# The heads stage of an RWKV-7 layer: gate projection moved, one identity matmul replaced by a VectorE add, dense k-tiles in rounds of three

## The chip, the cores and the metric

The kernel runs on one core of a Trainium2 chip. A core has five engines with their own instruction streams: TensorE (PE in the profile, its weight loads PEld), VectorE (DVE), ScalarE (ACT), GpSimd (POOL) and SyncE (SP, which here only issues DMAs). The engines wait for each other through semaphores; each works through its own instructions in a fixed order. The metric is the device time of one execution in microseconds (us), as a median of several runs.

## The reference

Two layers over 256 tokens of width 2048. Layer 0 mixes tokens by a short gated convolution, layer 1 by RWKV-7 time mixing; each is followed by a ConvFFN of width 5632. The part that matters here is the time mixing, with 32 heads of 64:

```
r, k, v = xr @ w_r, xk @ w_k, xv @ w_v
decay   = exp(-exp(-softplus(-(w0 + tanh(xw @ w1) @ w2)) - 0.5))
a       = sigmoid(a0 + (xa @ a1) @ a2)
g       = sigmoid(xg @ g1) @ g2
step:  S = S * w_t + (S @ -kk_t) (kk_t * a_t)^T + v_t k_t^T;   y_t = S @ r_t
y = groupnorm(y) * gn_g + gn_b + (sum(r * k * r_k)) * v
out = (y * g) @ w_o
```

So w, a and g each end in a product of a narrow hidden row (96, 96 and 256 wide) with a matrix of 2048 columns: these are the low-rank projections. The scan over 256 tokens is done in chunks of 64, which needs, for each head and chunk, the inverse of a 64x64 triangular matrix.

## The kernel before, in words

All products that need float32 accuracy are made of three matmuls in a reduced float32 form: a weight is split by ACT into a high part and by DVE into a low part (split_w, L136 and L137), and mm3 (L145 to L147) multiplies high by high, high by low and low by high. Weights come by SP in pieces of 1 MB into three raw buffers, and their two parts go into four buffers named hl.

The heads stage (rwkv_heads) works on pairs of heads: 16 pairs, called heads below, each 128 columns wide, on both halves of the 128 partitions. Four generators are its stages:

- stage0: the low-rank projections of w and a (tile "tl"), then 16 k-tiles of r and 16 of k into one PSUM bank "big" (group_a, which yields after every fourth k-tile: eight yields), and a copy to kr. These are the dense matmuls, 128x128 by 256 columns.
- stage1: norms of k, exponentials, and the four small products between the scaled a, b, k and r (tiles AR and BK). Its first matmul, L628, sums the squares.
- stage2: the inverse. Five levels double the inverted block. A level has two halves with a yield behind each: first X times L, scaled and masked on DVE into Tt (L711 and L713); then new X and new W in one bank of 512 columns, each made of an identity matmul that brings in the old value (L718) and eight 64x64 matmuls (L721), and one ACT copy of both to WX (L723). Then a correction (L728 to L743) gives W32.
- stage3: the matrix QT (L750, L752), the masked products FE (L757 and L759, masked on DVE at L762), the recurrence over four chunks (L772, L774), the output, group norm, the low-rank projection of the gate (gT, L802) and the product zf.

At step s, stage3 works on head s-3, stage2 on s-2, stage1 on s-1 and stage0 on s. Within a step the generators are called in turn, stage3 first, until all are done: one turn is a round. Stage2 has twelve rounds; stage0 has ten.

The code's order is only a priority: a list scheduler places instructions on each engine, and they keep that order on the chip. It can put a later round's dense matmul ahead, or break up a group. PSUM has eight banks: two each of the names "big", "tl", "inv" and "mn". The pool kx has two buffers a name, k1 one.

In the profile, AM and BR lie in a tile named xr0 (here xr_10226) and QT and FE in xr1 (xr_10227), so "mn<-xr,xr" at L759 is QT times BR, and "xr<-mn" at L762 is FE. The last three steps, with no stage0 left, are filled with the output projection's matmuls.

Of the kernel before, what the change touches and what calls it, by code (L numbers as in the profile page):

```python
# [11 lines left out]
F32 = mybir.dt.float32  # L12
# [69 lines left out]
def trunk(ctx: ExitStack, tc: tile.TileContext, x, ng, vec, cst, gnp, win, wout, up0, dn0, wl1, wv, wr, wk, wl2, wo,  # L82
# [87 lines left out]
    def group_a(src, xs, ps, j, cut=None):  # L170

        kt = 0
        ps = ps.rearrange("p (b t) -> p b t", b=NB)
        for hl in load_w(src, 1024 if KT >= 8 else KT * P, cut=cut):
            for i in range(min(8, KT)):
                c = i * P
                xh, xl = xs(kt, j)
                mm3(ps, hl[:, 0, c:c + P], hl[:, 1, c:c + P], xh, xl, kt == 0, kt == KT - 1)
                kt += 1
                if kt % 4 == 0:  # L180
                    yield
# [382 lines left out]
    def rwkv_heads(scr, xk, xr, lhid, ctxv, fill):  # L564
# [4 lines left out]
        with tc.tile_pool(name="kz", bufs=1, reuse_waits="tile") as zp, tc.tile_pool(name="kx", bufs=2, reuse_waits="tile") as kx, \  # L569
# [8 lines left out]
            def stage0(g, st):  # L578
                st.tw = kx.tile([P, T], F32, name="tw")
                st.ta = kx.tile([P, T], F32, name="ta")  # L580
                hl = load_w(wl2[g][:, :2 * P], 2 * P)[0]
                ps = bank("tl", 2, T)
                for w, dst in ((0, st.tw), (1, st.ta)):
                    mm3(ps[:, w], hl[:, 0, w * P:(w + 1) * P], hl[:, 1, w * P:(w + 1) * P], lhid[:, w, 0, :], lhid[:, w, 1, :],
                        True, True)
                    nc.scalar.activation(dst, ps[:, w], AF.Tanh, scale=0.5, bias=hb[:, w, g:g + 1])
                yield
                ps = bank("big", 2, T)
                yield from group_a(wr[g], xsel(xr), ps[:, 1], 0)
                yield from group_a(wk[g], lambda kt, j: (xk[kt // 4][:, :, kt % 4, 0, :], xk[kt // 4][:, :, kt % 4, 1, :]),  # L590
                                   ps[:, 0], 0)
                st.kr = kx.tile([P, 2, T], F32, name="kr")
                nc.scalar.activation(st.kr, ps, AF.Copy)
                yield
# [21 lines left out]
            def stage1(g, st):  # L616
# [47 lines left out]
                st.LM = kx.tile([P, NCC, CH], F32, name="LM")  # L664
# [32 lines left out]
            def stage2(g, st):  # L697
# [8 lines left out]
                WX, LT, LL = st.WX, st.LT, st.LL  # L706

                for li in range(len(LEVELS)):
                    ps = bank("inv", NCC, CH)
                    for c, s, R in pairs:  # L710
                        nc.tensor.matmul(ps[R, c], LT[R, c], WX[R, 1, c], start=True, stop=True)  # L711
                    Tt = kx.tile([P, NCC, CH], F16, name="Tt")
                    nc.vector.scalar_tensor_tensor(Tt, ps, 1.0 / NRES, bc(C_LV + 64 * li), ALU.mult, ALU.mult)  # L713
                    yield
                    ps = bank("inv", 2, NCC, CH)
                    for w in (1, 0):
                        for s, R in halves:
                            nc.tensor.matmul(ps[R, w], i16[R], WX[R, w], start=True, stop=False)  # L718
                        for c, s, R in pairs:
                            a, b = (WX[R, 0, c], Tt[R, c]) if w else (Tt[R, c], WX[R, 0, c])  # L720
                            nc.tensor.matmul(ps[R, w, c], a, b, start=False, stop=c == NCC - 1)  # L721
                    WX = kx.tile([P, 2, NCC, CH], F16, name="WX")
                    nc.scalar.activation(WX, ps, AF.Copy)  # L723
                    yield
# [4 lines left out]
                for s, R in halves:  # L729
                    nc.tensor.matmul(ps[R], i16n[R, 1], WX[R, 1], start=False, stop=False)  # L730
                for c, s, R in pairs:
                    nc.tensor.matmul(ps[R, c], LT[R, c], WX[R, 1, c], start=False, stop=False)
                    nc.tensor.matmul(ps[R, c], LL[R, c], WX[R, 1, c], start=False, stop=c == NCC - 1)
# [4 lines left out]
                for s, R in halves:  # L738
                    nc.tensor.matmul(ps[R], i16n[R, 0], WX[R, 0], start=True, stop=False)
                for c, s, R in pairs:  # L740
                    nc.tensor.matmul(ps[R, c], R16[R, c], WX[R, 0, c], start=False, stop=c == NCC - 1)
                st.W32 = kx.tile([P, NCC, CH], F32, name="W32")
# [3 lines left out]
            def stage3(g, st):  # L746
# [69 lines left out]
                nc.vector.tensor_tensor(out=grp(zf), in0=pt, in1=grp(gT), op=ALU.mult)  # L816
# [320 lines left out]
```

## Time and profile before

| what | value |
|---|---|
| median of three runs | 2610.01 us (2609.38 to 2610.29) |
| profiled execution | 2611.74 us, span 2610.0 us |
| PE busy | 2555.8 us, 98% of the span |
| DVE busy | 1696.1 us, 65% |
| ACT busy | 1348.1 us, 52% |
| granted TensorE clock | 0.995 |
| one step of the heads stage (L628 to L628) | 29.90 us |

The heads stage runs from about 1290 to 1790 us of the span. Times in the rows are in us from the span's start. In the timeline a row has its start, the time from the start of its first to the end of its last instruction, engine, line, operation, tiles, shape and count; for PE, "64*64" or "128*128" is the part of the array that a matmul uses. Matmuls overlap in the array, so that the distance of two starts, not the duration, is what one holds PE for. A group row ends with its busy time, the mean in ns of one instruction and the idle time before it.

### The profile page before, as it was taken

What the parts mean: (1) busy time and instruction counts of PE and PEld (TensorE: products, weight loads), DVE (VectorE), ACT (ScalarE), POOL (GpSimd) and SP (SyncE); (2) the same over time, 40 slices, a digit from 0 to 9 for tenths busy, and PEclk for the clock granted to TensorE, in tenths of its full rate; (3) what the DMA queues carried; (4) which work ended last, traced back from release to release, by engine and by line L of the source; (5) the groups of instructions that cost most, each with busy time, mean ns of one, the idle gap of its engine ahead of it and who ended that gap; (6) DMA issues with size and microseconds to landing.
All of it is one profiled execution on the core that took longest, in us unless ns stands there. A gap on an engine that the chain in (4) does not pass through costs nothing.

```text
span 2610.0 us, 44129 instructions
## 1 busy us (share of the span) xinstructions
PE 2555.8 (98%) x18284; PEld 2197.5 (84%) x18284; DVE 1696.1 (65%) x2365; ACT 1348.1 (52%) x2068; POOL 189.1 (7%) x255
## 2 busy tenths in 40 slices
PE   7999999999999999989999999999999999999998
PEld 7888888888888888868888888877888888888886
DVE  5666566667666645578756666665677776775555
ACT  5444455555555544469744444443555555554444
POOL 0000010000000000030222222320100000000000
PEclk9999999999999999999999999999999999999999
DMA  7555554555555555536523332335455555555553
GB/s 250 182 192 190 188 187 148 191 190 183 192 188 184 192 190 183 223 131 213 183 81 105 105 95 92 105 111 211 161 194 189 185 191 194 191 184 194 194 194 141
DMA packets 107417, 450.00 MB, mean 172 GB/s; under 512 B 29808, under 2 KB 47872, under 8 KB 57296
## 3 DMA queue, kind: packets, MB, share of 16 engines
q1 hardware_dynamic: 105760, 440.52, 48.1%
q0 software_dynamic: 1456, 6.66, 0.7%
q8 instruction: 143, 2.34, 0.3%
q14 instruction: 58, 0.48, 0.1%
HBM read 439.15 MB, written 8.00 MB: 171 GB/s over the span
## 4 chain that ended last, share of the span: by engine, by line
PE 76%; issue 18%; DVE 3%; ACT 1%; POOL 1%; DMA 0%; SPq 0%; DVEq 0%; POOLq 0%; ACTq 0%
PE tl L199 6%; PE big L199 6%; PE inv L199 6%; PE mn L199 6%; PE big L145 5%; PE big L146 4%; PE big L147 4%; PE tl L200 3%; PE big L200 3%; PE inv L200 3%; PE mn L200 3%; PE tl L145 2%; PE tl L147 2%; PE tl L146 2%; PE mn L146 2%
## 5 line engine op out<-in xcount | busy, mean ns | idle before, releaser
L137 DVE TENSOR_TENSOR hl<-raw,hl 128x1024 fp32r<-128x1024 f32 (+1 forms) x820 | 977.8, 1195 | 503.3 <-ACT hl L136 500.2
L136 ACT ACTIVATE hl<-raw 128x1024 fp32r<-128x1024 f32 (+1 forms) x820 | 843.5, 1031 | 575.9 <-PE big L147 151.0
L199 PE MATMUL big<-xhl,hl 128*128 128x512 f32 x880 | 309.4, 392 | 0.0
L199 PE MATMUL tl<-xhl,hl 128*128 128x512 f32 x880 | 309.4, 392 | 0.0
L199 PE MATMUL mn<-xhl,hl 128*128 128x512 f32 x864 | 303.9, 392 | 0.0
L199 PE MATMUL inv<-xhl,hl 128*128 128x512 f32 x864 | 303.6, 392 | 0.0
L200 PE MATMUL big<-xhl,hl 128*128 128x256 f32 x880 | 246.0, 280 | 0.0
L200 PE MATMUL tl<-xhl,hl 128*128 128x256 f32 x880 | 246.0, 280 | 0.0
L200 PE MATMUL mn<-xhl,hl 128*128 128x256 f32 x864 | 241.5, 279 | 0.0
L200 PE MATMUL inv<-xhl,hl 128*128 128x256 f32 x864 | 241.4, 279 | 0.0
L199 PEld LDWEIGHTS big<-xhl,hl 128*128 128x128 f32 x880 | 164.8, 187 | 38.0
L199 PEld LDWEIGHTS tl<-xhl,hl 128*128 128x128 f32 x880 | 164.7, 187 | 38.0
L199 PEld LDWEIGHTS inv<-xhl,hl 128*128 128x128 f32 x864 | 161.7, 187 | 37.3
L199 PEld LDWEIGHTS mn<-xhl,hl 128*128 128x128 f32 x864 | 161.8, 187 | 37.1
L200 PEld LDWEIGHTS big<-xhl,hl 128*128 128x128 f32 x880 | 165.5, 188 | 0.0
L200 PEld LDWEIGHTS tl<-xhl,hl 128*128 128x128 f32 x880 | 165.5, 188 | 0.0
L200 PEld LDWEIGHTS mn<-xhl,hl 128*128 128x128 f32 x864 | 162.4, 188 | 0.0
L200 PEld LDWEIGHTS inv<-xhl,hl 128*128 128x128 f32 x864 | 162.4, 188 | 0.0
L308 POOL TENSOR_TENSOR r<-s,nhalf 128x1 f32<-128x1 f32 x16 | 8.9, 554 | 1234.9 <-DVE s L306 1234.9
L145 PE MATMUL big<-xr,hl 128*128 128x256 f32 x268 | 83.0, 310 | 0.0
L145 PE MATMUL big<-xkv,hl 128*128 128x256 f32 x256 | 78.1, 305 | 0.0
L146 PE MATMUL big<-xr,hl 128*128 128x256 f32 x268 | 77.3, 288 | 0.0
(517 smaller groups left out, 5008.4 us busy)
## 6 DMA issues: line engine op xcount, KB each, us to landing
raw<-in_up_dram SPq DMA_DIRECT2D x172, 1024.0 KB, 4.8
raw<-in_dn_dram SPq DMA_DIRECT2D x88, 1024.0 KB, 4.8
raw<-in_win_dram SPq DMA_DIRECT2D x46, 1024.0 KB, 4.9
raw<-in_wout_dram SPq DMA_DIRECT2D x16, 1024.0 KB, 4.8
raw<-in_wv_dram SPq DMA_DIRECT2D x16, 1024.0 KB, 4.9
raw<-in_wr_dram SPq DMA_DIRECT2D x16, 1024.0 KB, 4.9
raw<-in_wk_dram SPq DMA_DIRECT2D x16, 1024.0 KB, 4.9
raw<-in_wo_dram SPq DMA_DIRECT2D x16, 1024.0 KB, 5.2
```

What stands on the lines that cost most here:

```text
L136: nc.scalar.activation(hl[:, 0, C], s[:, C], AF.Copy)
L137: nc.vector.tensor_tensor(out=hl[:, 1, C], in0=s[:, C], in1=hl[:, 0, C].bitcast(F32), op=ALU.subtract)
L145: nc.tensor.matmul(o, wh, xh, start=start, stop=False)
L146: nc.tensor.matmul(o, wh, xl, start=False, stop=False)
L147: nc.tensor.matmul(o, wl, xh, start=False, stop=stop)
L199: nc.tensor.matmul(ps, hl[:, 0, W], xhl[:, kt], start=kt == 0, stop=False)
L200: nc.tensor.matmul(ps[:, 1], hl[:, 1, W], xhl[:, kt, 0], start=False, stop=kt == KT - 1)
L308: nc.gpsimd.tensor_tensor(out=r, in0=s, in1=nhalf[:, 0:1], op=ALU.pow)
```

## The change

Four edits, all in the heads stage.

1. Spread: group_a yields after every third k-tile, with an offset, so that the 32 k-tiles of r and k take eleven rounds (three each, the last two k-tiles in the twelfth), and stage0 has twelve rounds like stage2.
2. Gate: the gate's low-rank projection moves from stage3 to stage0. One load of four panels replaces two loads of two; its product goes through a "big" bank; gT gets four buffers because it is used three steps later.
3. Old X by VectorE: X and W have tiles of their own. X's new value is eight matmuls in one bank, to which DVE adds the old X (one instruction, 128x256, from PSUM and SBUF into float16). W keeps its identity matmul and gets an ACT copy of 256 columns.
4. LM and W32 get one buffer instead of two.

```diff
-    def group_a(src, xs, ps, j, cut=None):
+    def group_a(src, xs, ps, j, first=4, step=4):
...
-                if kt % 4 == 0:
+                if kt % step == first % step:
                     yield
...
-                hl = load_w(wl2[g][:, :2 * P], 2 * P)[0]
+                hl = load_w(wl2[g], 4 * P)[0]
...
-                yield
+                ps = bank("big", 512)[:, :T]
+                for k in (2, 3):
+                    mm3(ps, hl[:, 0, k * P:(k + 1) * P], hl[:, 1, k * P:(k + 1) * P], lhid[:, k, 0, :], lhid[:, k, 1, :],
+                        k == 2, k == 3)
+                st.gT = kx.tile([P, T], F32, name="gT", bufs=4)
+                nc.scalar.activation(st.gT, ps, AF.Copy)
                 ps = bank("big", 2, T)
-                yield from group_a(wr[g], xsel(xr), ps[:, 1], 0)
+                yield
+                yield from group_a(wr[g], xsel(xr), ps[:, 1], 0, 3, 3)
                 yield from group_a(wk[g], lambda kt, j: (xk[kt // 4][:, :, kt % 4, 0, :], xk[kt // 4][:, :, kt % 4, 1, :]),
-                                   ps[:, 0], 0)
+                                   ps[:, 0], 0, 2, 3)
...
-                st.LM = kx.tile([P, NCC, CH], F32, name="LM")
+                st.LM = k1.tile([P, NCC, CH], F32, name="LM")
...
-                    ps = bank("inv", 2, NCC, CH)
-                    for w in (1, 0):
-                        for s, R in halves:
-                            nc.tensor.matmul(ps[R, w], i16[R], WX[R, w], start=True, stop=False)
-                        for c, s, R in pairs:
-                            a, b = (WX[R, 0, c], Tt[R, c]) if w else (Tt[R, c], WX[R, 0, c])
-                            nc.tensor.matmul(ps[R, w, c], a, b, start=False, stop=c == NCC - 1)
-                    WX = kx.tile([P, 2, NCC, CH], F16, name="WX")
-                    nc.scalar.activation(WX, ps, AF.Copy)
+                    Xn = kx.tile([P, NCC, CH], F16, name="X")
+                    ps = bank("inv", NCC, CH)
+                    for c, s, R in pairs:
+                        nc.tensor.matmul(ps[R, c], W[R, c], Tt[R, c], start=True, stop=True)
+                    nc.vector.tensor_tensor(out=Xn, in0=ps, in1=X, op=ALU.add)
+                    Wn = kx.tile([P, NCC, CH], F16, name="W")
+                    ps = bank("inv", NCC, CH)
+                    for s, R in halves:
+                        nc.tensor.matmul(ps[R], i16[R], W[R], start=True, stop=False)
+                    for c, s, R in pairs:
+                        nc.tensor.matmul(ps[R, c], Tt[R, c], W[R, c], start=False, stop=c == NCC - 1)
+                    nc.scalar.activation(Wn, ps, AF.Copy)
+                    W, X = Wn, Xn
                     yield
...
-                st.W32 = kx.tile([P, NCC, CH], F32, name="W32")
+                st.W32 = kx.tile([P, NCC, CH], F32, name="W32", bufs=1)
...
-                hl = load_w(wl2[g][:, 2 * P:], 2 * P)[0]
-                ps = bank("mn", 512)
-                for k in range(2):
-                    mm3(ps[:, :T], hl[:, 0, k * P:(k + 1) * P], hl[:, 1, k * P:(k + 1) * P], lhid[:, 2 + k, 0, :],
-                        lhid[:, 2 + k, 1, :], k == 0, k == 1)
-                gT = k1.tile([P, T], F32, name="gT")
-                nc.scalar.activation(gT, ps[:, :T], AF.Copy)
```

Line numbers shift with the change. The ones used below, before and after: L628 and L635 (sums of squares), L711 and L718 (X times L), L713 and L720 (Tt), L718 and L730 (identity, after the change for W alone), L721 and L725 (X's product) or L732 (W's), L750 and L761 (QT), L757 and L768, L759 and L770 (FE's products), L762 and L773 (FE's masks), L772 and L783 (recurrence), L774 and L785 (its state on DVE); new is L726 (X's add).

How the scheduler's order moves is seen at two places. The first is PE at the start of a step, around the tanh inputs of w and a (tl<-lhid). Before:

```order
L145 MATMUL big<-xr,hl 128x256
L145 MATMUL tl<-lhid,hl 128x256
L146 MATMUL tl<-lhid,hl 128x256
L750 MATMUL mn<-xr_10226,W_13714 64x128 x8
L147 MATMUL tl<-lhid,hl 128x256
L757 MATMUL mn<-AR_10229,BK_10231 128x128
L718 LDWEIGHTS i_10221
L718 MATMUL inv<-WX_13425,i_10221 64x256
```

After the change, from the end of the gate's matmuls to the second tanh input:

```order
L147 MATMUL big<-lhid,hl 128x256
L768 MATMUL mn<-AR_10229,BK_10231 128x128
L770 MATMUL mn<-xr_10226,xr_10227 128x128
L768 MATMUL mn<-AR_10229,BK_10231 128x128
L635 MATMUL tl<-csts,sq 128x2 x2
L145 MATMUL tl<-lhid,hl 128x256
L146 MATMUL tl<-lhid,hl 128x256
L147 MATMUL tl<-lhid,hl 128x256
L770 MATMUL mn<-xr_10226,xr_10227 128x128
L768 MATMUL mn<-AR_10229,BK_10231 128x128
L770 MATMUL mn<-xr_10226,xr_10227 128x128
L145 MATMUL tl<-lhid,hl 128x256
```

QT (L750, now L761) is made ahead of the step's L635, and FE's products start ahead of it and stand on both sides of the tanh inputs, where before they came behind them. After the second tanh input ten of FE's sixteen products are left, then one level's matmuls, nine dense ones and the recurrence (L783); before, those were all sixteen, one level's matmuls and five dense ones.

The second place is DVE in the same part of a step. Before:

```order
L631 TENSOR_SCALAR ri<-tl 128x4
L623 TENSOR_SCALAR tw<-tw 128x256
L713 SCALAR_TENSOR_TENSOR Tt<-inv,hc 128x256
L137 TENSOR_TENSOR hl<-raw,hl 128x1024
L762 TENSOR_TENSOR xr_10227<-mn,hc 128x512 x2
L653 TENSOR_TENSOR AR_10228<-kr,Pt 128x4x64
L774 TENSOR_SCALAR SV<-mn,pc 64x64 x2
```

After:

```order
L638 TENSOR_SCALAR ri<-tl 128x4
L630 TENSOR_SCALAR tw<-tw 128x256
L137 TENSOR_TENSOR hl<-raw,hl 128x1024
L773 TENSOR_TENSOR xr_10227<-mn,hc 128x512 x2
L726 TENSOR_TENSOR X<-inv,WX_16144 128x256
L785 TENSOR_SCALAR SV<-mn,pc 64x64 x2
L660 TENSOR_TENSOR AR_10228<-kr,Pt 128x4x64
```

The split of weights (L137) still stands directly ahead of the masks of FE; Tt has gone from this place, and X's add stands between the masks and the recurrence's state.

More of the change, by code (lines that the diff above doesn't have):

```diff
@@ L168, in bank8 @@
         return bank(next(turn), *shape)
-    def group_a(src, xs, ps, j, cut=None):
+    def group_a(src, xs, ps, j, first=4, step=4):
         kt = 0
         ps = ps.rearrange("p (b t) -> p b t", b=NB)
-        for hl in load_w(src, 1024 if KT >= 8 else KT * P, cut=cut):
+        for hl in load_w(src, 1024 if KT >= 8 else KT * P):
             for i in range(min(8, KT)):
@@ L586, in stage0 @@
                     nc.scalar.activation(dst, ps[:, w], AF.Tanh, scale=0.5, bias=hb[:, w, g:g + 1])
+                ps = bank("big", 512)[:, :T]
[4 more added lines that the diff above has]
+                nc.scalar.activation(st.gT, ps, AF.Copy)
+                ps = bank("big", 2, T)
                 yield
-                ps = bank("big", 2, T)
-                yield from group_a(wr[g], xsel(xr), ps[:, 1], 0)
+                yield from group_a(wr[g], xsel(xr), ps[:, 1], 0, 3, 3)
                 yield from group_a(wk[g], lambda kt, j: (xk[kt // 4][:, :, kt % 4, 0, :], xk[kt // 4][:, :, kt % 4, 1, :]),
-                                   ps[:, 0], 0)
+                                   ps[:, 0], 0, 2, 3)
                 st.kr = kx.tile([P, 2, T], F32, name="kr")
@@ L705, in stage2 @@
                     nc.sync.dma_start(st.V[R], v)
-                WX, LT, LL = st.WX, st.LT, st.LL
+                W, X, LT, LL = st.WX[:, 0], st.WX[:, 1], st.LT, st.LL
                 for li in range(len(LEVELS)):
@@ L710, in stage2 @@
                     for c, s, R in pairs:
-                        nc.tensor.matmul(ps[R, c], LT[R, c], WX[R, 1, c], start=True, stop=True)
+                        nc.tensor.matmul(ps[R, c], LT[R, c], X[R, c], start=True, stop=True)
                     Tt = kx.tile([P, NCC, CH], F16, name="Tt")
@@ L729, in stage2 @@
                 for s, R in halves:
-                    nc.tensor.matmul(ps[R], i16n[R, 1], WX[R, 1], start=False, stop=False)
+                    nc.tensor.matmul(ps[R], i16n[R, 1], X[R], start=False, stop=False)
                 for c, s, R in pairs:
-                    nc.tensor.matmul(ps[R, c], LT[R, c], WX[R, 1, c], start=False, stop=False)
-                    nc.tensor.matmul(ps[R, c], LL[R, c], WX[R, 1, c], start=False, stop=c == NCC - 1)
+                    nc.tensor.matmul(ps[R, c], LT[R, c], X[R, c], start=False, stop=False)
+                    nc.tensor.matmul(ps[R, c], LL[R, c], X[R, c], start=False, stop=c == NCC - 1)
                 R16 = kx.tile([P, NCC, CH], F16, name="R16")
@@ L738, in stage2 @@
                 for s, R in halves:
-                    nc.tensor.matmul(ps[R], i16n[R, 0], WX[R, 0], start=True, stop=False)
+                    nc.tensor.matmul(ps[R], i16n[R, 0], W[R], start=True, stop=False)
                 for c, s, R in pairs:
-                    nc.tensor.matmul(ps[R, c], R16[R, c], WX[R, 0, c], start=False, stop=c == NCC - 1)
-                st.W32 = kx.tile([P, NCC, CH], F32, name="W32")
+                    nc.tensor.matmul(ps[R, c], R16[R, c], W[R, c], start=False, stop=c == NCC - 1)
+                st.W32 = kx.tile([P, NCC, CH], F32, name="W32", bufs=1)
                 nc.scalar.activation(st.W32, ps, AF.Copy, scale=1.0 / NRES)
@@ L815, in stage3 @@
                 zf = k1.tile([P, T], F32, name="zf")
-                nc.vector.tensor_tensor(out=grp(zf), in0=pt, in1=grp(gT), op=ALU.mult)
+                nc.vector.tensor_tensor(out=grp(zf), in0=pt, in1=grp(st.gT), op=ALU.mult)
                 if fill.zhl is None:
```

## The prediction

> **What bounds the kernel now.** I read the page's engine shares first, then the table of stretches for three whole steps of the heads stage (the only stage the change touches), then who waits there, and last the timeline of TensorE (PE), VectorE (DVE) and ScalarE (ACT) within one step.
>
> ```profile
> PE 2555.8 (98%) x18284; PEld 2197.5 (84%) x18284; DVE 1696.1 (65%) x2365; ACT 1348.1 (52%) x2068; POOL 189.1 (7%) x255
> ```
>
> ```profile
> 1394.20:1424.10 29.90, 29.89 (x459) 26.47 (x457) 19.84 (x42) 14.15 (x30) 8.28 (x11) 1.00 0.30 96
> 1513.80:1543.70 29.90, 29.89 (x459) 26.46 (x457) 19.83 (x42) 14.16 (x30) 8.28 (x11) 1.00 0.31 97
> ```
>
> These rows give a stretch, its length, the busy time of PE, PEld, DVE, ACT and POOL, the granted clock, the DMA share and GB/s. Each stretch is one step, from one L628 (the squared norms of a head, stage 1's first matmul) to the next. Two steps four apart take the same 29.90 us, with PE busy for 29.89, the clock at 1.00 and the DMA engines at 0.30. So PE's own sequence of matmuls sets the step, and 16 heads pass through it at 29.90 us each. DVE is idle for a third of it.
>
> ```profile
> POOL cc L688 <- PE mn L772: 67.0, 10, 6.7
> ...
> PEld big L145 <- issue: 3.4, 20, 0.2
> ```
>
> In the table of waits over ten steps (total us, times, longest), the longest PE entry is 3.4 us, 0.34 us a step. There is little waiting to win back; what the change gains or loses must be PE work, or a new wait.
>
> **The change part by part.** *The identity matmuls.* Per level, a step has two pairs of L718 (one for X, one for W) and two groups of eight L721.
>
> ```profile
> 1499.14 0.83 PE L779 MATMUL mn<-SV,xr 64*64 64x64 f32 x16
> 1499.90 0.30 PE L718 MATMUL inv<-WX,i 64*64 64x256 f16 x2
> 1500.03 0.29 PE L721 MATMUL inv<-Tt,WX 64*64 64x64 f16 x8
> 1500.16 0.28 PE L718 MATMUL inv<-WX,i 64*64 64x256 f16 x2
> 1500.27 0.29 PE L721 MATMUL inv<-WX,Tt 64*64 64x64 f16 x8
> 1500.39 1.07 PE L676 MATMUL tl<-BK,AR 64*64 64x128 f32 x16
> ```
>
> Durations overlap, so I take starts: an L718 pair holds PE for 0.11 to 0.13 us. One pair less for five levels is 5 x 0.11 = 0.55 us a step saved.
>
> *More blocks of dense k-tiles.* The dense matmuls (L145 to L147) fill the 128x128 array; their neighbours run as 64*64, 64*128 or 128*64. Here is one dense block of twelve, with its neighbours, and one entry from an f16 group:
>
> ```profile
> 1494.20 0.29 PE L721 MATMUL inv<-WX,Tt 64*64 64x64 f16 x8
> 1494.41 0.39 PE L145 MATMUL big<-xr,hl 128*128 128x256 f32 x1
> ...
> 1497.51 0.39 PE L145 MATMUL big<-xr,hl 128*128 128x256 f32 x1
> 1497.73 0.28 PE L146 MATMUL big<-xr,hl 128*128 128x256 f32 x1
> 1497.85 0.28 PE L147 MATMUL big<-xr,hl 128*128 128x256 f32 x1
> ...
> 1498.93 0.28 PE L147 MATMUL big<-xr,hl 128*128 128x256 f32 x1
> ```
>
> Within a block the starts are 0.12 apart. The first matmul holds PE for 0.22, so 0.10 extra; the last one, at 1498.93, is followed by L779 at 1499.14, 0.21 later, so 0.09 extra; and the L721 group before the block holds 0.21 instead of the 0.12 it takes ahead of L718, so 0.09 more. A dense block costs 0.12 a matmul and 0.28 for being a block. Counting the order of one steady step, PE enters the full array from a smaller tiling 12 times before and 15 times after (rounds of three k-tiles instead of four, dense work in the two rounds that had little, and the gate's six matmuls as a block where they were glued to a k-tile block). That is 3 x 0.28 = 0.84 us. The sixteen matmuls of L757 and L759 lose the L718/L721 group in their middle and get three dense pieces in its place; what is not in the blocks I bound by 0 and 0.3 and take 0.1, since two changes among the small tilings fall away and broken pairs come in. PE work per step: -0.55 + 0.84 + 0.10 = +0.39 us.
>
> In the Trainium skill, the page "TensorEngine Tiling (Array Packing)", Key Properties, says that changing the tiling mode drains TensorE. The rows agree that a change costs and put it near 0.09 us a side. The Trainium skill's page "TensorE: Matmul & The Clock Gate" (Part 2, Single matmul latency) puts a drain at about 175 ns; by that, as an estimate, two sides of three blocks would be 1.05 us a step instead of the rows' 0.84, and the time some 3 us later.
>
> *A new wait at the state recurrence.* At the start of a step the recurrence's first matmul (L772, after the change L783) needs both halves of FE, which DVE masks (L762) after the last L759; ahead of them in DVE's queue stands a split of weights (L137).
>
> ```profile
> 1483.90 0.61 PE L628 MATMUL tl<-csts,sq 128*128 128x2 f32 x4
> ...
> 1484.89 0.31 PE L741 MATMUL inv<-WX,R 64*64 64x64 f16 x8
> ...
> 1486.98 0.38 PE L147 MATMUL tl<-lhid,hl 128*128 128x256 f32 x1
> 1487.30 0.48 PE L757 MATMUL mn<-AR,BK 64*128 64x128 f32 x2
> ...
> 1489.73 0.38 PE L759 MATMUL mn<-xr,xr 64*128 64x128 f32 x2
> 1490.04 0.21 PE L721 MATMUL inv<-Tt,WX 64*64 64x64 f16 x1
> ...
> 1491.20 0.58 PE L772 MATMUL mn<-SV,xr 64*64 64x64 f32 x3
> 1491.52 0.28 PE L711 MATMUL inv<-WX,LT 64*64 64x64 f16 x6
> 1491.62 0.22 PE L772 MATMUL mn<-SV,xr 64*64 64x64 f32 x1
> ```
>
> ```profile
> 1486.74 0.42 ACT L641 ACTIVATE sq<-ri 128x256 f32<-128x256 f32 x1 [0.99 <-POOL ri L632]
> 1487.59 0.47 ACT L586 ACTIVATE ta<-tl,hb 128x256 f32<-128x256 f32 x1
> 1487.95 1.06 ACT L136 ACTIVATE hl<-raw 128x1024 fp32r<-128x1024 f32 x1
> 1489.04 1.23 DVE L137 TENSOR_TENSOR hl<-raw,hl 128x1024 fp32r<-128x1024 f32 x1 [2.88 <-ACT hl L136]
> 1490.18 1.28 DVE L762 TENSOR_TENSOR xr<-mn,hc 128x512 f32<-128x512 f32 x2
> 1491.88 0.60 DVE L774 TENSOR_SCALAR SV<-mn,pc 64x64 f32<-64x64 f32 x2
> ```
>
> From the end of the last tanh input (1486.98 + 0.38 = 1487.36) to the end of the second mask (1490.18 + 1.28 = 1491.46) runs one chain of queues, 4.1 us: tanh on ACT, then the split's two halves on ACT and DVE, then the masks. Today L759 ends at 1490.11, just when the split does, so the masks lose nothing; PE arrives at L772 at 1491.20 and the second half goes at 1491.62, some 0.3 us late, partly filled with L711.
>
> After the change most of L757/L759 (now L768/L770) is pulled ahead of and around the tanh inputs, but the split and the masks keep their place in DVE's queue behind the same chain. From the step's start (L628, now L635, at 0) in PE's new order: 0.99 for L628 and three dense (1483.90 to 1484.89); 13 of the 16 L757/L759 at 0.15 (sixteen took 2.4 us between 1487.30 and 1490.04 without the L718 and L721 among them), 1.95; three dense as a block, 3 x 0.12 + 0.28 = 0.64; one level's X and W matmuls, 0.36; nine dense, 9 x 0.12 + 0.28 = 1.36. PE reaches the recurrence at 5.3. The tanh input ends near 0.99 + 3 x 0.15 + 0.64 = 2.1; plus 4.1 the masks are done at 6.2, and up to 6.4 as ACT may also have the copy that spreads ri (L641, 0.42) in that place. PE waits about 0.9 to 1.1 us there instead of 0.3: +0.6 to +0.8, and I take 0.65, near the lower end, as the second half of L783 can go after the first.
>
> *What else is on DVE.* X is now added on DVE, five times a step.
>
> ```profile
> L207 DVE TENSOR_TENSOR s<-tl,s 128x256 f32<-128x256 f32 x44 | 18.7, 425 | 38.0 <-ACT s L206 38.0
> L723 ACT ACTIVATE WX<-inv 128x512 f16<-128x512 f32 x50 | 29.5, 591 | 17.5 <-PE inv L721 17.5
> L735 ACT ACTIVATE R<-inv 128x256 f16<-128x256 f32 x10 | 3.8, 379 | 0.0
> L713 DVE SCALAR_TENSOR_TENSOR Tt<-inv,hc 128x256 f16<-128x256 f32 x50 | 21.0, 419 | 0.6
> L137 DVE TENSOR_TENSOR hl<-raw,hl 128x1024 fp32r<-128x1024 f32 x41 | 49.9, 1217 | 34.7 <-ACT hl L136 34.7
> L137 DVE TENSOR_TENSOR hl<-raw,hl 128x256 fp32r<-128x256 f32 x20 | 9.1, 455 | 1.9 <-ACT hl L136 1.6
> ```
>
> The nearest rows for an add of a PSUM tile of 256 are L207 and L713, 0.42 us: DVE gets 5 x 0.42 = 2.1 us, 19.84 to 21.9 of a step; ACT's copy falls from 0.59 to L735's 0.38, 1.06 us less. Neither engine sets the step, so both cost nothing while PE's dense block covers them: a round has X or Tt out of PE (0.3), DVE (0.42) and some 0.1 between engines, 0.8 us, under a block of 9 x 0.12 + 0.28 = 1.36 where 12 x 0.12 + 0.28 = 1.72 stood. With a split of 1.23 ahead of it the same round takes up to 2.0, so the cover fails in rounds that have little else; I put 0 to 0.5 us a step and take 0.05.
>
> *The gate's move.* One load of four panels replaces two of two; its split is one of 512 columns for two of 256 (0.45 each on DVE), the same work. Its ACT copy stays one per head. Sixteen DMAs fewer on SP, at a DMA share of 0.30, cost and save nothing. The bank "big" now serves the gate and the k and r sums in turn, so the next head's first k-tile must wait until ACT has copied kr; in the new order that copy is due some four us before, so nothing. Single buffers for LM and W32 free before their next write for the same reason: they are read within the round or two behind it.
>
> **Sum.** Per step +0.39 work, +0.65 at the recurrence, +0.05 in the rounds: +1.1 us. Each of 16 heads passes once: +17 us, from the profiled execution's 2611.7 us (span 2610.0) to 2629; the runs' median is 2610.0, 1.7 lower, so I predict 2627.
>
> **The rivals.** *DVE becomes the bound in the short rounds.* Where a split stands ahead of Tt or of X's add, 2.0 - 1.36 = 0.6 us is lost. Two such hand-overs in a step's ten cost 1.2 us, 19 us over the heads, on top of the forecast: 2646. For it speaks that four splits of 1.22 a step (41 in ten steps, in the rows above) share DVE's queue with ten such hand-overs; against it that other stages' matmuls stand in most rounds too. It decides once a round's cover falls under 1.4 us.
>
> *Cover wins (the other side).* If the 0.10 at a block's first matmul is no price of the block but a late weight or bank, three blocks cost 0.54 instead of 0.84; and if dense work in every round also removes the 0.34 of waits and the masks come ahead of the split in time, the step is -0.55 + 0.54 + 0.10 - 0.34 = -0.25, and up to -0.8 if the small group's exposed start (L741 to L759, six us with only twelve dense matmuls) tightens: 2597 to 2606. It decides when the masks end before PE reaches L783. Against it: the 0.10 stands in every block quoted, whatever is ahead of it.
>
> *A wash.* The work as above, but the new wait no longer than today's 0.3: +0.39 less the 0.34 of old waits, 16 x 0.05 = 1 us: 2611. For it: the new order might let the split start before the tanh, since ACT's queue is half idle. Against it: the order has the split's DVE half ahead of the masks.
>
> **How the numbers follow.** Forecast 0.66; short rounds on DVE 0.16; cover wins 0.08; a wash 0.10. Under 0.2% (5 us) cannot be told from no change here. So faster 0.08, same 0.10, slower 0.82. The forecast's own range takes the work term's bounds (+0.3 to +0.6) and the wait's (+0.3 to +1.0): 16 x 0.6 to 16 x 1.6, 2620 to 2636. Reaching to the wash below and into the DVE case above, until no more than 0.2 is left out, gives 2610 to 2640.
>
> **What would show it.** A step from L635 to L635 near 31.0 us instead of 29.90; PE's sum of work without waits up by 0.4; L783 starting about 0.9 us after the dense block before it has ended, with DVE's masks directly behind a split; L726 at 0.42. The prediction is wrong if the steps are at or under 29.9, if L783 follows its block at once, or if the loss sits in L718 and L725 waiting for Tt and X.

## The result, and the profile after

| | before | after |
|---|---|---|
| median | 2610.15 us (2609.38 to 2610.46, 4 runs) | 2625.18 us (2623.9 to 2626.82, 4 runs) |
| ratio to before | | 1.0057, 95% interval 1.0042 to 1.0072 |
| profiled execution, span | 2611.74 us, 2610.0 us | 2624.08 us, 2622.3 us |
| steady step of the heads stage | 29.90 us | 30.74 us |

The change made the kernel 15.0 us slower; 2627 was predicted. In two experiments below, the gate alone and the add with the gate, one execution each ran at a granted clock of 0.75 and 0.60 and took 3119 and 3861 us; they move the medians given there by 0.7 us at most, and the ratios leave them out. First the engine shares on the page of after, then its table of stretches for two steady steps (columns as in the prediction's).

```profile
PE 2565.3 (98%) x18124; PEld 2201.8 (84%) x18124; DVE 1717.3 (65%) x2429; ACT 1332.7 (51%) x2052; POOL 188.8 (7%) x255
```

```profile
1397.90:1428.65 30.75, 30.29 (x447) 26.61 (x446) 21.27 (x46) 13.22 (x29) 8.19 (x11) 1.00 0.29 94
1520.84:1551.59 30.75, 30.29 (x448) 26.61 (x447) 21.27 (x46) 13.22 (x29) 8.19 (x11) 1.00 0.29 94
```

PE has 160 matmuls fewer, as it should, but is busy 9.5 us longer in the span. In a step it is busy for 30.29 of 30.75 us, where it was busy for 29.89 of 29.90: 0.40 more, and a new gap of 0.46. The 0.40 is not work alone. A matmul counts as busy to its modelled end, so a part of what PE waits stands as busy; summed by starts, in the table further down, the work is only 0.05 more and the waits 0.78. The clock stands at 1.00 in both and the DMA share at 0.30 and 0.29. The table of waits over ten steps names the gap (total us, times, longest):

```profile
PEld mn L783 <- DVE xr L773: 8.0, 20, 0.4
...
PE mn L783 <- DVE xr L773: 4.6, 20, 0.3
...
PEld big L145 <- issue: 3.4, 20, 0.2
```

The recurrence's matmuls (L783) and their weight loads wait for FE's masks (L773), twice in every step. Neither row has a counterpart before, and no wait for Tt (L720) or X's add (L726) is among PE's waits. The place in the timeline, PE first and then ACT and DVE:

```profile
1520.84 0.61 PE L635 MATMUL tl<-csts,sq 128*128 128x2 f32 x4
...
1524.24 0.38 PE L770 MATMUL mn<-xr,xr 64*128 64x128 f32 x2
...
1525.03 0.39 PE L145 MATMUL big<-xr,hl 128*128 128x256 f32 x1
...
1526.09 0.28 PE L147 MATMUL big<-xr,hl 128*128 128x256 f32 x1
1526.56 0.32 PE L783 MATMUL mn<-SV,xr 64*64 64x64 f32 x2 [0.19 <-DVE xr L773]
1527.16 0.33 PE L783 MATMUL mn<-SV,xr 64*64 64x64 f32 x2 [0.27 <-DVE xr L773]
1527.41 0.44 PE L656 MATMUL tl<-csts,sq 128*128 128x128 f32 x2
```

```profile
1523.24 0.46 ACT L587 ACTIVATE ta<-tl,hb 128x256 f32<-128x256 f32 x1
1523.60 1.05 ACT L136 ACTIVATE hl<-raw 128x1024 fp32r<-128x1024 f32 x1
1524.68 1.23 DVE L137 TENSOR_TENSOR hl<-raw,hl 128x1024 fp32r<-128x1024 f32 x1 [1.93 <-ACT hl L136]
1525.82 1.28 DVE L773 TENSOR_TENSOR xr<-mn,hc 128x512 f32<-128x512 f32 x2
1527.02 0.41 DVE L726 TENSOR_TENSOR X<-inv,WX 128x256 f16<-128x256 f32 x1
```

FE's last product ends at 1524.62, but the masks start at 1525.82, when the split ahead of them in DVE's queue ends; DVE itself stood idle for 1.93 us ahead of that split. The masks end at 1527.10. PE could have gone on at 1526.30 (0.21 after its last dense start) and leaves the place at 1527.41.

To see the whole step by kind of work, I add up the distances from each matmul's start to the next one's, as a mean over eight steady steps (us). What PE waits stands with the kind ahead of the wait; the dense row is shown without the wait that the block of nine ahead of L783 holds (1.525 us there, 1.265 in a block of nine that waits for nothing).

| kind of work on PE | before | after | difference | predicted |
|---|---|---|---|---|
| levels (L718, L721; after L725, L730, L732) | 2.767 | 2.196 | -0.57 | -0.55 |
| dense (L145 to L147), without the wait | 15.395 | 15.699 | +0.30 | +0.84 |
| FE's products (L757, L759; after L768, L770) | 2.400 | 2.815 | +0.42 | +0.10 |
| QT (L750; after L761) | 1.021 | 0.924 | -0.10 | 0 |
| wait ahead of the recurrence, in the dense row | 0 | 0.260 | +0.26 | with the next |
| recurrence (L772; after L783), its own waits with it | 0.864 | 1.384 | +0.52 | +0.65 for both |
| all others | 7.453 | 7.455 | 0.00 | +0.05 |
| step | 29.90 | 30.73 | +0.83 | +1.1 |

The fifteen distances from one L635 to the next are 14.7 us longer in sum: eleven steady steps take 9.2 of it, the first three (filling the pipeline) 3.3 and the last (emptying it) 2.2. Outside them the profiled execution is 2.4 us shorter; I have no cause for that. The granted clock explains neither. Within the fifteen distances it stood at 1.00 after the change (before, it was 0.93 in the second step). Over the whole span it was a little lower after, 0.992 against 0.995, and 0.85 in the stretch behind the last distance (1736.24 to 1770.00 us).

Last the groups of after by line (busy us, mean ns of one, idle before), over ten steps:

```profile
L726 DVE TENSOR_TENSOR X<-inv,X 128x256 f16<-128x256 f32 x40 | 16.7, 417 | 0.3
...
L733 ACT ACTIVATE W<-inv 128x256 f16<-128x256 f32 x50 | 19.0, 379 | 54.6 <-PE inv L732 53.5
...
L660 DVE TENSOR_TENSOR AR<-kr,Pt 128x256 f32<-128x256 f32 x10 | 4.3, 426 | 0.3
```

X's add takes 0.417 us and W's copy 0.379, as L207 and L735 promised. (L660 is shown for an experiment below.)

### The profile page after: what moved, and what is told of

The parts are those of the page before. It is cut to its first block, busy times and chain, and to the rows that moved or that the text cites. A ratio compares the mean times of both kernels' runs of the same rounds, so it can differ in the third digit from the quotient of the medians.

```text
span 2622.3 us, 43773 instructions
## 1 busy us (share of the span) xinstructions
PE 2565.3 (98%) x18124; PEld 2201.8 (84%) x18124; DVE 1717.3 (65%) x2429; ACT 1332.7 (51%) x2052; POOL 188.8 (7%) x255
## 4 chain that ended last, share of the span: by engine, by line
PE 71%; issue 20%; ACT 3%; DVE 3%; POOL 2%; SPq 0%; DMA 0%; DVEq 0%; POOLq 0%; ACTq 0%
PE tl L200 6%; PE big L200 6%; PE inv L200 6%; PE mn L200 6%; PE big L145 5%; PE big L147 4%; PE big L146 4%; PE tl L201 3%; PE inv L201 3%; PE big L201 3%; PE mn L201 3%; PE inv L147 2%; PE inv L146 2%; PE inv L145 2%; PE tl L145 2%
## 5 line engine op out<-in xcount | busy, mean ns | idle before, releaser
L137 DVE TENSOR_TENSOR hl<-raw,hl 128x1024 fp32r<-128x1024 f32 (+1 forms) x804 | 974.6, 1214 | 481.8 <-ACT hl L136 477.1
L145 PE MATMUL big<-xr,hl 128*128 128x256 f32 x268 | 84.1, 314 | 0.0
L145 PE MATMUL big<-xkv,hl 128*128 128x256 f32 x256 | 79.4, 310 | 0.0
L147 PE MATMUL big<-xr,hl 128*128 128x256 f32 x268 | 76.9, 287 | 0.0
```

The costliest lines, as they stand in the source:

```text
L137: nc.vector.tensor_tensor(out=hl[:, 1, C], in0=s[:, C], in1=hl[:, 0, C].bitcast(F32), op=ALU.subtract)
L145: nc.tensor.matmul(o, wh, xh, start=start, stop=False)
L147: nc.tensor.matmul(o, wl, xh, start=False, stop=stop)
```

## The experiments

Theory: PE's own sequence sets the step; the loss is a wait of the recurrence for masks that stand behind a split of weights, and work in more and broken pieces, which what the identity matmuls save nearly pays for. The rivals: VectorE has become the bound in short rounds; or the gate's move or the add is itself the loss. The experiments first take the change apart, then take the split away from the masks, and then put together what pays.

Each time is a median beside runs of the kernel before on the same chip; the ratio has its 95% interval. Line numbers shift a little from kernel to kernel; the text says what each is. All keep LM and W32 with one buffer, but for the one that is the kernel before with one edit.

### The add alone

Of the change only the third and fourth edit: X's add on DVE, single buffers. The gate stays in stage3 and the k-tiles in fours.

```diff
-                yield from group_a(wr[g], xsel(xr), ps[:, 1], 0, 3, 3)
+                yield from group_a(wr[g], xsel(xr), ps[:, 1], 0)
...
-                                   ps[:, 0], 0, 2, 3)
+                                   ps[:, 0], 0)
...
-                st.gT = kx.tile([P, T], F32, name="gT", bufs=4)
...
+                gT = k1.tile([P, T], F32, name="gT")
```

> Only X's add moves to VectorE (tiles W and X apart, single buffers for LM and W32); the gate stays in stage3, four k-tiles a round. Theory (the loss is dense blocks plus the wait of the recurrence for FE's masks behind a weight split; X's add itself is the gain): the order still has 12 entries into the full array, the identity pairs are gone, so PE's work per step falls by 0.57 us; some of it is lost in waits for Tt and X, step 29.4 to 29.5 instead of 29.90, time 2604 to 2610. Rival (VectorE's added 2.1 us per step makes Tt, X and the masks late, and that is the loss): step 30.5 or more, time 2619 to 2626.

Measured: 2604.23 us against 2610.54, ratio 0.9978 (0.9969 to 0.9988). A step takes 29.41 us. The levels fall from 2.767 to 2.374, so 0.18 less than in after: FE's products still break up one level here, whose three groups hold 0.70 us in pieces, where the same level holds 0.48 in after. A Tt comes late once a step besides, as one block of twelve ahead of L719 shows, which holds 1.85 us where the others hold 1.62. The recurrence falls from 0.864 to 0.659. This part by itself is a gain.

### The gate alone

Before, with the gate's projection in stage0 and single buffers.

```diff
-                hl = load_w(wl2[g][:, :2 * P], 2 * P)[0]
+                hl = load_w(wl2[g], 4 * P)[0]
...
+                st.gT = kx.tile([P, T], F32, name="gT", bufs=4)
...
-                gT = k1.tile([P, T], F32, name="gT")
```

> Only the gate's projection moves to stage0; old X stays an identity matmul, four k-tiles a round. Theory: the order changes at the step's start, QT waits for W32 or the masks come late; laying the trace's durations along the new order gives 0.8 us a step more, nearly all wait, 2618 to 2622. Rival (the gate's move costs nothing, the add or the spread does it all): 2609 to 2612.

Measured: 2618.2 us against 2610.54, ratio 1.0035 (1.0022 to 1.0048); a step of 30.57 us. In the sums by kind the loss stands at the dense matmuls (15.395 to 16.335), because the wait comes behind one. PE and ACT in its timeline (L759 is QT, L752 ACT's copy to W32, L648 the copy that spreads ri, L587 the tanh):

```profile
1518.04 0.31 PE L750 MATMUL inv<-WX,R 64*64 64x64 f16 x8
...
1518.90 0.28 PE L147 MATMUL big<-xr,hl 128*128 128x256 f32 x1
1520.39 1.09 PE L759 MATMUL mn<-xr,W 64*64 64x128 f32 x16 [1.21 <-ACT W L752]
```

```profile
1517.91 0.47 ACT L587 ACTIVATE tw<-tl,hb 128x256 f32<-128x256 f32 x1 [0.40 <-PE tl L147]
1519.65 0.41 ACT L648 ACTIVATE sq<-ri 128x256 f32<-128x256 f32 x1 [1.26 <-POOL ri L639]
1519.97 0.37 ACT L752 ACTIVATE W<-inv 128x256 f32<-128x256 f32 x1
```

W32's matmuls end at 1518.35, but their copy stands in ACT's queue behind L648, which waits 1.26 us for GpSimd. PE waits 1.21 us for the copy. In the kernel before the same two stand the other way round:

```profile
1485.38 0.38 ACT L743 ACTIVATE W<-inv 128x256 f32<-128x256 f32 x1
1486.74 0.42 ACT L641 ACTIVATE sq<-ri 128x256 f32<-128x256 f32 x1 [0.99 <-POOL ri L632]
```

So "the gate's move costs nothing" does not hold for the move alone: its matmuls and its copy cost nothing, but the order that the scheduler makes of it has put a waiting instruction ahead of one that PE needs. In after this wait isn't there, since QT is made ahead of L635.

### The spread alone

Before, with three k-tiles a round and single buffers.

```diff
-                if kt % 4 == 0:
+                if kt % step == first % step:
                     yield
...
-                yield from group_a(wr[g], xsel(xr), ps[:, 1], 0)
+                yield from group_a(wr[g], xsel(xr), ps[:, 1], 0, 3, 3)
```

> Only three k-tiles a round instead of four over twelve rounds. Theory: more dense blocks and broken FE products cost PE work, 0.5 to 0.7 us a step, no new wait at the recurrence: 2618 to 2622. Rival (a block has no price of its own, spread hides waits): 2605 to 2611.

Measured: 2623.74 us against 2610.54, ratio 1.0053 (1.0041 to 1.0065); a step of 30.78 us. The spread alone costs nearly as much as the whole change. The expectation missed: the time lies above its range, and the loss is not where it was sought. Its sums by kind: FE +0.30, recurrence +0.24, levels +0.49, dense -0.06, QT -0.10. So the dense blocks cost nothing in net, and beside FE's broken pieces it is waits that make the step longer, at the recurrence too, where none was expected. Its waits over ten steps:

```profile
PEld mn L775 <- DVE xr L765: 3.6, 10, 0.4
...
PEld L723 <- issue: 3.1, 10, 0.3
...
PE mn L775 <- DVE xr L765: 2.2, 10, 0.2
```

L775 is the recurrence, which waits for the masks here too. L723 is X's product in a level. Its row names no releaser, but the timeline does:

```profile
1419.49 0.42 DVE L715 SCALAR_TENSOR_TENSOR Tt<-inv,hc 128x256 f16<-128x256 f32 x1
```

```profile
1419.96 0.31 PE L723 MATMUL inv<-Tt,WX 64*64 64x64 f16 x8
```

Tt ends at 1419.91 and L723 starts right behind it; PE had started the identity pair at 1419.51, and in the other levels X's product follows the pair after 0.10 to 0.13, not 0.44. So one short round does lose some 0.3 us a step to DVE here, which is what the first rival named.

### The add and the gate, without the spread

The changed kernel with the k-tiles in fours.

```diff
-                yield from group_a(wr[g], xsel(xr), ps[:, 1], 0, 3, 3)
+                yield from group_a(wr[g], xsel(xr), ps[:, 1], 0)
...
-                                   ps[:, 0], 0, 2, 3)
+                                   ps[:, 0], 0)
```

> The change without its spread: gate in stage0, X's add on VectorE, four k-tiles a round. Theory: 12 entries instead of 15, the work of the identity pairs saved, waits for Tt and X up by some 0.4: step 29.5 to 29.8, 2606 to 2612. Rival (VectorE's add is the loss, spread is not): 2620 to 2626, as the whole change.

Measured: 2606.65 us against 2610.54, ratio 0.9986 (0.9977 to 0.9995). The step, 29.07 us, is the shortest of all kernels here, so eleven steady steps gain 9.1 us; yet the median gains 3.9. In the profiled execution (2611.55 us, 4.9 over the median) the first step takes 23.81 us instead of before's 19.54. A good part of that is the granted clock. The first step in the profile of this kernel, and the same step in after's:

```profile
1289.98:1313.79 23.81, 21.28 (x215) 19.42 (x214) 12.39 (x21) 9.16 (x19) 6.58 (x8) 0.86 0.45 145
```

```profile
1288.66:1309.89 21.23, 18.69 (x215) 16.95 (x214) 12.27 (x21) 9.27 (x19) 6.68 (x8) 1.00 0.46 147
```

PE has 215 matmuls in both and is busy 2.6 us longer at a clock of 0.86; in the kernel with the gate alone, also in fours, this step takes 21.15 us at 1.00. The clock was down again behind the last step (0.76 from 1717.48 to 1746.00 us, against 1.00 in before's stretch from 1721.99 to 1755.00). So the steady step is a gain, and in this execution a part of it was lost to the clock in the first steps and behind the last; why the clock fell there was not tried. Against after, taking the spread away is worth some 19 us.

### The spread and the gate, without the add

The changed kernel with old X and W both brought in by identity matmuls and one ACT copy.

```diff
-                    nc.vector.tensor_tensor(out=Xn, in0=ps, in1=X, op=ALU.add)
...
+                    for w in (1, 0):
+                        for s, R in halves:
+                            nc.tensor.matmul(ps[R, w], i16[R], WX[R, w], start=True, stop=False)
```

> The whole change without X's add: spread and gate stay, old X comes by identity matmuls into the bank of 512 as before. Theory (the add is a gain): PE's work per step higher by 0.3 to 0.57 us, part of it given back in waits; step 30.7 to 31.0, 2624 to 2629. Rival (the add on VectorE is what makes the change slow): 2610 to 2618.

Measured: 2625.04 us against 2609.70, ratio 1.0054 (1.0041 to 1.0067), a step of 30.71 us: the same as after. Beside the other two parts the add is worth nothing, although the levels are 0.53 shorter with it (2.725 without, 2.196 with). The dense row is 0.31 shorter without the add (15.649 against 15.959) and the recurrence 0.23 (1.151 against 1.384). Its waits over ten steps (L781 is the recurrence, L771 the masks):

```profile
PEld mn L781 <- DVE xr L771: 6.9, 20, 0.4
...
PE mn L781 <- DVE xr L771: 2.7, 10, 0.3
```

The wait is there without the add, and grows with it: PE's total goes from 2.7 to 4.6 and PEld's from 6.9 to 8.0. One of the five shorter levels stands between FE's products and the recurrence, so PE is only earlier at a place where it waits: the block ahead of the recurrence and its first group hold 1.41 + 0.62 us without the add and 1.53 + 0.85 with it, 0.35 more. The other 0.19 is the price of one more dense block (15 in after's step, 14 here).

### The add and the spread, without the gate

The changed kernel with the gate's projection in stage3.

```diff
-                hl = load_w(wl2[g], 4 * P)[0]
+                hl = load_w(wl2[g][:, :2 * P], 2 * P)[0]
...
-                st.gT = kx.tile([P, T], F32, name="gT", bufs=4)
...
+                gT = k1.tile([P, T], F32, name="gT")
```

> X's add and three k-tiles a round; the gate stays in stage3. Theory (the spread is the part that costs, whatever stands beside it): FE's products broken up and waits for Tt, step 30.5 to 30.9, 2621 to 2628. Rival (spread costs only with the gate in stage0 or with the old identity matmuls): 2604 to 2612.

Measured: 2629.69 us against 2610.67, ratio 1.0074 (1.0061 to 1.0088); a step of 31.09 us, slightly over what was expected. Its waits over ten steps (L777 is the recurrence, L767 the masks, L712 X times L, L720 X's add):

```profile
PEld mn L777 <- DVE xr L767: 7.5, 20, 0.4
PE inv L712 <- DVE X L720: 5.5, 10, 0.6
PEld L712 <- issue: 5.2, 10, 0.5
...
PE mn L777 <- DVE xr L767: 2.7, 10, 0.3
```

The wait for the masks is there as in after. A second one has come, 0.55 us a step, for X's add in one short round.

Together with before and after these are all eight combinations (difference of the medians to before, us):

| | neither add nor gate | add | gate | add and gate |
|---|---|---|---|---|
| k-tiles in fours | 0 | -6.3 | +7.7 | -3.9 |
| spread | +13.2 | +19.0 | +15.3 | +15.0 |

The spread costs in every column, from 7.6 us (beside the gate) to 25.3 (beside the add). The add saves 6.3 and 11.6 in fours and costs 5.8 or saves 0.3 with the spread. The gate costs 7.7 alone and saves 4.0 beside the two others. Each difference has an interval of 2 to 4 us to either side, so the 0.3 is no difference, and those of 4 or less are hardly clear of the noise. The parts don't add up: each decides where the waits of the others fall.

### The split taken away from the masks

The changed kernel, but from the fourth head on the low part of k's second weight piece, the split that stands ahead of FE's masks, is subtracted by GpSimd.

```diff
-            nc.vector.tensor_tensor(out=hl[:, 1, C], in0=s[:, C], in1=hl[:, 0, C].bitcast(F32), op=ALU.subtract)
+            (low or nc.vector).tensor_tensor(out=hl[:, 1, C], in0=s[:, C], in1=hl[:, 0, C].bitcast(F32), op=ALU.subtract)
...
-                                   ps[:, 0], 0, 2, 3)
+                                   ps[:, 0], 0, 2, 3, low=(1,) if g > 2 else ())
```

> The whole change; in addition, from the fourth head on, the low part of k's second weight piece (the split that stands ahead of FE's masks in VectorE's queue) is subtracted on GpSimd instead of VectorE. Theory: the masks then start when FE's products end, the recurrence waits no longer, and a step loses 0.7 to 1.2 us of its 30.74, 12 to 13 steps of it: 2609 to 2616. Rival (the loss is only dense blocks and VectorE is not concerned): 2622 to 2627. If GpSimd's subtraction (some 3 us from its 1.55 us for 512 columns) comes too late for k's second half, PE waits there and it is slower: 2630 or more.

And the same edit to the kernel before, to see what it is worth where the masks lose nothing:

> The kernel before with the same split's low part on GpSimd from the fourth head on. It is the control for e5: the recurrence waits only some 0.15 to 0.3 us a step here. Theory: 2605 to 2609, a gain of 1 to 5 us and a third or less of e5's. Rival (taking a split from VectorE helps everywhere alike): as large a gain as in e5.

Measured: the changed kernel 2612.19 us against 2609.70, ratio 1.0011 (1.0003 to 1.002), a step of 29.90; the kernel before 2607.3 us, ratio 0.9989 (0.998 to 0.9998), a step of 29.65. The edit is worth 12.5 us on the changed kernel (+15.0 to +2.5, each against the kernel before beside it) and 2.4 on the kernel before; per step 0.84 against 0.25. Both waits for the masks have gone from the changed kernel's table of PE's waits, of which only this row is left over ten steps:

```profile
PEld big L145 <- issue: 3.4, 20, 0.2
```

This is the loss that was predicted at the recurrence: of the 15 us some 10 (12.5 less 2.4) go with a split that no longer stands ahead of the masks. It isn't a pure subtraction of the wait, for two reasons. The scheduler made another order, with 14 entries into the full array for 15, which is worth 0.20 a step. And there is a new loss. The wait that goes is 0.26 ahead of L783 and 0.82 in its first group (0.854 to 0.037), so with the block 1.28 us a step are won, but the step is only 0.84 shorter. PE, POOL (GpSimd) and DVE in its timeline:

```profile
1526.59 0.60 PE L783 MATMUL mn<-SV,xr 128*64 128x64 f32 x4
```

```profile
1523.31 2.37 POOL L137 TENSOR_TENSOR hl<-raw,hl 128x1024 fp32r<-128x1024 f32 x1 [0.48 <-ACT hl L136]
```

```profile
1522.92 1.29 DVE L773 TENSOR_TENSOR xr<-mn,hc 128x512 f32<-128x512 f32 x2 [1.59 <-PE mn L770]
1524.13 0.41 DVE L726 TENSOR_TENSOR X<-inv,WX 128x256 f16<-128x256 f32 x1
1524.46 1.50 DVE L660 TENSOR_TENSOR AR<-kr,Pt 128x256 f32<-128x256 f32 x1
1525.88 0.41 DVE L664 TENSOR_TENSOR BK<-kr,kf 128x256 f32<-128x256 f32 x1
1526.22 0.59 DVE L785 TENSOR_SCALAR SV<-mn,pc 64x64 f32<-64x64 f32 x2
```

The masks now run at once. But L660, which takes 0.43 us in after, takes 1.50: it ends 0.28 us after GpSimd's subtraction (1525.68). The recurrence's state L785 stands behind it, ends at 1526.81, and the second L783 group holds PE for 0.73 us where the third holds 0.27. So 0.46 us a step of what the edit won is lost again, which makes up the sum (1.28 less 0.46 is 0.82); a version without this collision could, as an estimate, take 29.4 a step.

### The add alone, with the split on GpSimd

The first experiment's kernel with the last one's edit; both gained by themselves.

```diff
-                                   ps[:, 0], 0)
+                                   ps[:, 0], 0, low=(1,) if g > 2 else ())
```

> X's add alone (as e1) with the one split's low part on GpSimd from the fourth head on (as e5 and e6). Theory: the recurrence's remaining wait for the masks goes, 0.1 to 0.25 us a step as in e6, on top of e1's 2604.2: 2600 to 2603, under both kernels. Rival (e1 has no such wait left to give): 2604 to 2606.

Measured: 2602.96 us against 2610.67, ratio 0.9972 (0.9963 to 0.9981), a step of 29.31. It is the fastest kernel of this study, 7.7 us under the kernel before, though its interval overlaps that of the add alone.

### Both adds on VectorE

The last kernel, with W's old value brought in by a DVE add as well; no identity matmul is left in the levels.

```diff
-                    for s, R in halves:
-                        nc.tensor.matmul(ps[R], i16[R], W[R], start=True, stop=False)
...
-                    nc.scalar.activation(Wn, ps, AF.Copy)
+                    nc.vector.tensor_tensor(out=Wn, in0=ps, in1=W, op=ALU.add)
```

> The version of e1 (X's add alone), with W's old value also added by VectorE (no identity matmul and no ScalarE copy in the levels) and the split of e5 on GpSimd. Theory: another 5 pairs less, 0.55 us of PE work a step, against some 0.6 more of waits for Tt, X and W as VectorE gets 5 x 0.42 more and one split of 1.2 less; 2597 to 2603, under e1's 2604. Rival (VectorE is full by then, its queue sets the step): 2606 to 2615.

Measured: 2606.69 us against 2609.70, ratio 0.9986 (0.9977 to 0.9995), a step of 29.50 us: a miss, 3.7 us over the last kernel instead of under it. A second pair of identity matmuls a level should have taken 0.55 us more from the levels; they fell by 0.11 only (2.374 to 2.263), the dense row rose by 0.35 (15.397 to 15.746) and the recurrence by 0.155. The time saved came back as waits, but only the smaller of the two is for DVE. PE's waits over ten steps (L762 is FE's product with QT, L755 ACT's copy of QT, L712 X times L, L720 X's add), and ACT ahead of that copy (L642 is the copy that spreads ri):

```profile
PE mn L762 <- ACT xr L755: 4.5, 10, 0.5
PE inv L712 <- DVE X L720: 2.3, 10, 0.2
```

```profile
1510.27 0.41 ACT L642 ACTIVATE sq<-ri 128x256 f32<-128x256 f32 x1 [1.83 <-POOL ri L633]
1510.59 0.58 ACT L755 ACTIVATE xr<-mn 128x512 f32<-128x512 f32 x1
```

The larger, 0.45 us a step, stands in the levels' row, as PE stops in the middle of a level's matmuls. It is the loss of the gate alone over again: the copy that PE needs stands in ACT's queue behind one that waits for GpSimd, here 1.83 us where it waits 0.33 in the last kernel. The other, 0.23 us, is X's add. So the time lies in the rival's range, but the trace does not show a DVE that sets the step: the larger loss comes of the order that the scheduler made for ACT and GpSimd.

## Why the prediction was right, and where its sizes were off

**The bound was right.** PE's sequence sets the step: in the steady steps its clock (1.00), the DMA share (0.30 and 0.29) and the time of all other kinds of work (7.45 both times) did not move, and the added time is all PE's work and PE's waits.

**The work: too high.** +0.39 was said; the rows by kind give +0.05 (-0.57, +0.30, +0.42 and -0.10). PE's busy time did rise by 0.40 as forecast, but that agreement is luck, since a part of it is waiting that counts as busy. Nearly all of the loss is the wait.

**The identity matmuls: right.** -0.57 us a step for -0.55.

**The dense blocks and FE's pieces: 0.22 too high together, and split wrongly.** Blocks +0.84 and FE +0.10 make +0.94; the rows have +0.30 and +0.42, so +0.72. A block's own rows hold 0.16 to 0.20 beyond its 0.12 a matmul, mostly 0.19, in before and after alike, as the prediction had it (0.10 in and 0.09 out); the third share, 0.09 at the group ahead, stands in the table with that group, and here FE's products are often that group. So the FE term was mis-sized (+0.10 against +0.42) because entries that were charged to the blocks fall on FE's rows, and, as I read the order, because more of its pairs are broken than assumed. And the prediction overlooked that two blocks before held 0.14 and 0.09 more than the price, which after's blocks don't; that takes 0.23 from the three new ones (3 x 0.19 = 0.57, less 0.23, is near the 0.30). What one isolated block costs was read from rows, not tried in a run of its own.

**QT: not foreseen.** Sixteen L761 hold PE for 0.924 instead of 1.021. No dense matmul comes right behind them any more (before L147 did, after L718 does), which fits the 0.09 that a small group pays ahead of a block. The prediction counted QT as unchanged.

**The wait at the recurrence: right in place and cause, a little low.** The prediction let PE reach the recurrence at 5.3 us of the step and the masks end at 6.2 to 6.4. In the timeline PE could start L783 at 5.46 (1526.30 less 1520.84) and the masks end at 6.26. Ahead of L783 and in its first group PE loses 1.08 us where 0.9 to 1.1 was said. For the difference to before +0.65 was taken, the lower end of 0.6 to 0.8; the rows have 0.26 + 0.52 = +0.78. The split on GpSimd shows the cause: with the split gone from the masks' way the wait goes, and with it 12.5 us on the changed kernel against 2.4 on the kernel before. The sign that was named for it, L783 some 0.9 us behind its block, came in another form: L783 starts 0.26 us late, and the other 0.82 us are lost inside its first group, whose second half waits for the second mask.

**The rounds: right for this kernel, by a narrow margin.** No wait for Tt or X's add is among after's PE waits, against 0.05 predicted. But with the spread alone one Tt costs 0.3 us a step, and with add and spread one X costs 0.55, near the 0.6 that the rival put on a hand-over. The mechanism of that rival is real; the order of the full change just misses it: once a step X's add ends 0.09 us, and once a Tt 0.05 to 0.06 us, ahead of the matmul that reads it.

**The gate: "nothing" held in the full change, not for the part.** Alone it costs 7.7 us, of which the wait through ACT's queue shows in the trace. Beside the two other parts it saves 4.0; beside one of them it costs 2.1 (spread) or 2.4 (add), within the noise. The prediction looked at the gate's own copies and buffers and not at what the new order puts ahead of W32's copy. (One split of 512 columns takes DVE 0.68 us where two of 256 took 0.91, so the work is less, not the same.)

**The sum.** +0.83 a step instead of +1.1: the work is 0.34 under its term and the rounds 0.05, the wait 0.13 over. Sixteen times 0.83 would be 13.3 us. In the profiled executions the first three steps and the last lost more than a steady one (5.5 us in four instead of 3.3), and 2.4 came back outside; the medians are 15.0 apart. So the total (2625 for 2627) is nearer than the step, and that is luck: the terms erred in both directions, and the first and last steps, which the prediction did not cost apart, made up for a part of the work that did not come.

**The rivals.** "Cover wins" and "a wash" needed masks that end before PE arrives; they end 0.8 us after it. Against "cover wins" stands too that the blocks of after, too, cost 0.17 to 0.20 in their own rows. For "a wash" 2611 was said. As an estimate from the rows by kind, 29.90 + 0.05 = 29.95 us a step would have come of the change without the longer wait, so its figure was a fair one for the condition that failed. The kernel with the split on GpSimd comes near it (2612), but by another sum: one block fewer, and the new loss behind L660.

## What to carry to other kernels

When work is reordered to keep the bounding engine busy, follow the queues of the helping engines past the new places: an instruction that waits (a split for its other half, a copy for another engine) holds up all that stands behind it, and four of the losses here (masks behind a split, W32's copy and QT's copy behind a waiting copy, X's add in a short round) are of that kind. Count how many blocks a finer interleaving makes, since each costs at both ends, and measure the parts of a change alone and together, because a part that gains alone (0.11 us of PE for 0.42 us of DVE) can be worth nothing where PE already waits for DVE at the next place. And read a busy share with care: some of PE's waiting counted as busy here, and the sums of starts told it apart.

## What the runs showed of the hardware that I had not expected

While GpSimd subtracted 128x1024 elements (2.37 us; DVE takes 1.23 for the same), a DVE operation on two SBUF tiles of 128x256 (L660) took 1.50 us instead of 0.43 and ended 0.28 us after GpSimd's. The group over ten steps shows that it is so every time:

```profile
L660 DVE TENSOR_TENSOR AR<-kr,Pt 128x256 f32<-128x256 f32 x10 | 15.1, 1512 | 0.0
```

DVE operations with one operand in PSUM kept their times beside it: the masks L773 two in 1.29 us (1.28 in after) and X's add L726 0.41. In the Trainium skill, the page "SBUF — State Buffer", section "Who interferes with whom", says that a DVE instruction with two SBUF inputs contends with a GpSimd instruction that reads SBUF; it calls the ports that they share an exclusive lock, so that the later one blocks. This trace agrees: 1.50 us against 0.43, and no such loss where an input is in PSUM.
